# A two-layer attention trunk on one core: the opening's four hand-written orders replaced, nine modulation rows on TensorE instead of twelve, x in six loads instead of five

## The chip, the core and the metric

The kernel runs on one core of a Trainium2 chip. The core has a matrix engine (TensorE, PE in the profile, with its weight loads listed as PEld), a vector engine (DVE), a scalar engine (ACT), GpSimd (POOL) and a queue engine (SP), from which nearly all of this kernel's DMAs are issued. The metric is the device time of one execution in microseconds. It is compared with the time of the kernel before, run on the same chip.

## The reference

Two layers on 512 tokens of width 2048. The first is differential attention, the second forgetting attention on keys, values and gates that are projected once between them; each layer ends in a layer norm. All is float32. The change lies in the beginning of the first layer: its modulation, and the projection of its first two heads.

```python
def reference(x, c, w_mod, b_mod, ...):
    c_act = jax.nn.silu(c)
    for l in range(DEPTH):                                   # DEPTH = 2
        mod = c_act @ w_mod[l] + b_mod[l]                    # (1, 6144)
        shift, scale, gate = jnp.split(mod, 3, axis=-1)
        h = x * (1.0 + scale[:, None]) + shift[:, None]      # (1, 512, 2048)
        if l < N_A:
            y = diff_attention(h, a_w_in[l], a_w_out[l], ...)    # h @ w_in: 2048 to 8192, softmax, values, gate, @ w_out
        else:
            ...
            y = forgetting_attention(h, b_w_in[l - N_A], b_w_out[l - N_A], k_sh, v_sh, F_sh)
        x = layer_norm(DN_ALPHA * x + gate[:, None] * y, ln_g[l], ln_b[l])
    return x
```

`h` needs all 2048 rows of the first 4096 columns of `w_mod[0]` (33.6 MB) before its last column is there.

## The kernel before

A float32 product is made of three matmuls. Each operand is split into a high part, rounded to the matrix engine's faster 32-bit format, and the low rest: `hh` and `hl` for the activations, `whi` and `wlo` for the weights. A product is hh x whi + hl x whi + hh x wlo. ACT makes the high part of a weight block from its staged load (`wst` to `whi`, line 118), DVE the low part (`wlo`, line 125).

The opening is everything up to the end of the projections of heads 0 and 1. The 2048 rows of the contraction are 16 k-tiles of 128, and it does these things at once:

- The modulation. `sms` tiles hold pieces of `w_mod`, loaded on SP (step L, line 557). The k-tiles are grouped into nine sets: the first two hold one k-tile each, the other seven two. A set sums 16 blocks of 128 weight rows, here called rows. A row is either added on DVE into `sacc` (step d, lines 605 and 607) or multiplied on PE by the column `cact` straight into PSUM (step e, line 635, a group that a matmul of a zero mask opens, line 632). `PE_ROWS` says which rows are PE's. Once all rows of a set are there, PE sums `sacc` over the partitions into the same PSUM columns (step o, line 649) and DVE adds the bias: `mcol`, shift and scale (step m, line 660).
- The activations. `x` comes in quarters of 512 columns, the first in two parts (step X, line 567). PE transposes a k-tile (step t, line 675; the first into a bank called `px`), ACT applies scale and shift twice (`hh`, step h, line 683; `htmp`, step i, line 690), and DVE makes `hl` from the two (step l, line 698).
- The products. Weight blocks of two k-tiles are loaded on SP into four staging buffers (step W, line 59, two loads each), cast on ACT (step a) and finished on DVE (step b). Blocks of 384 columns and of 512 columns alternate for each head. A k-tile of a head is seven accumulations, three for the first block (banks called `sc` and `o` in the profile) and four for the second (`acc`), each of three matmuls, steps A (hh x whi), B (hl x whi) and C (hh x wlo), line 709: 672 in all. Both heads share seven PSUM banks and take turns in seven phases; ACT stores a bank's sums (step c, line 750) and loads them back (step r, line 759).
- Two matmuls of a constant tile (step F, line 621), whose result nothing reads.

What each of SP, ACT, PE and DVE does first and next is written out by hand in four strings (`ORDER_SP`, `ORDER_ACT`, `ORDER_PE`, `ORDER_DVE`): a letter is the next step of its kind, a number ahead of it repeats it. Steps that a string leaves out go to its end, as step p does in the kernel before (`load_parameters`, seven small loads of layer norm weights, lambda vectors and a gain that are used after the opening). Each engine runs its own string strictly in order and waits wherever something is not there yet. A modulation tile may be loaded when the tile five before it has been read (`NBUF`), a weight block when DVE is done with the block four before it.

After the opening the rest follows in program order: the remaining heads, the output projection, the shared keys and values, the second layer.

Of the kernel before, what the change touches and what calls it, by code (L numbers as in the profile page):

```python
# [16 lines left out]
P = 128  # L17
D = 2048
KT = D // P
T = 512  # L20
# [9 lines left out]

PHASES = [(0, 0, 2), (1, 0, 4), (0, 2, 6), (1, 4, 10), (0, 6, 14), (1, 10, 16), (0, 14, 16)]
KMAJOR = (0,)
PE_ROWS = {0: (2, 3, 6, 7), 1: (4, 5, 6, 7, 12, 13, 14, 15)}
EARLY = (0,)
NBUF = 5
ORDER_SP = '8LX4LW4LXW2LW4LW3LW2LW5L2W2LX2W4LW4LW3LW2LW3LXWLWLW2L2W5LWLW4LWLWLXW3LWL2WL2WL6W'
ORDER_ACT = 'haiahia5ca2cahiahi3c2rara2c2r2c2rahiahica2c2rc2r2c2rcahirahi2ahihia2cac3ra3c2rc2rahi2ahiahaihi2acrcrcra2crc2racrahihi3a2crc2rcarcr2c2r7c'
ORDER_PE = 'F4eFto3eAeA4eBoAtBCB2ACBACBACB2ACBC3ABC2B2AC2B3CAB2C3ABACBABABC3B2AC2BCA2CoBAtCACBA2C2Bt3ACAB3AB2CA4B2CBCACBCBCB2CAB2C3ABCACBA3BCABC4A3BoCA2CABA3CA2B2CB2At3AB2C2BCtCABA2B5AC2BA2C3BCA2C2B2CBAB2ACB3CBCA2CBCBABC2ACoB2ABABACtBCAB2ACBCtBAC2BC2ABCBAB2C2ABABACB2CB4A2B2CA2CBCABA3B2CAoABt3CBC2A2CBAtAC4BABCACA2CAB3ABCA2CBACBABACA2B2CA3BCA2CABACAC2BC2BABC2A2BACABCB2A2Bo2AC2AtCBACBCBC2ACA2BACA2BABCBCA2CBCA2C3BACACBCtAB2CA2B2ACABABCACAoCACA2C3BABCBtBCBA2BCA3CBAtBAB2C4A2C2ABCACB2CABA2BACAB2CB2A2BC2BACB4CBCAB3ACBABABC2B2CB2CAB2ACBCAB2C2ABABCBA2CB2ABABAoBCBAt2ACAC2AB3C2BABAt2B3CA4BACABA3CACABAB3CBCBAB4CA2BAB2A3CBA2BACBA2CBC2A2BC2A2B2A3CABCBACBA2B3ABAB3C2B5CABACBC'  # L40
ORDER_DVE = '13dm2dbl5dmb2dbl14dbm4dlbdl2db9dbdb2dmdbl3dldb10dmb5db3dldbl5dbm2dbl2dl4db2db6db3dm6dbdb2dl4dlb3dmb3db2ld2bdb3db5dmlbl4b'
MANUAL = {ET.DVE, ET.PE, ET.Activation, ET.SP}
CUT = False
LAM_INIT = 0.8 - 0.6 * math.exp(-0.0)
# [93 lines left out]
def tile_yoco(  # L138
# [44 lines left out]
    def acc_bank(name="acc"):  # L183
        return ps.tile([P, 512], F32, name=name, tag="acc", bufs=4)
# [4 lines left out]
    def tr_bank(name="tr"):  # L189
        return ps.tile([P, 512], F32, name=name, tag="tr", bufs=1)  # L190
# [105 lines left out]
    first = {h: (Job(a_w_in, [(256 * h, 256), (2048 + 256 * h, 128)]), vg[h]) for h in range(2)}  # L296
    kk = Job(a_w_in, [(2048 + 128, 128), (2048 + 384, 128)])

    sets = [(0, 1), (1, 1)] + [(k, 2) for k in range(2, KT, 2)]
    phases = PHASES  # L300
    kj = [Job(kv_w, [(512 * g, 512)]) for g in range(4)]

# [174 lines left out]
    with tc.tile_pool(name="start", bufs=2, reuse_waits="tile") as sp, tc.manual_schedule(engines=MANUAL):  # L477
# [5 lines left out]
        for i, (k0, nk) in enumerate(sets):  # L483
            nr = 8 // nk
# [2 lines left out]

        loads = []
        for n, (i, k, nr) in enumerate(tiles):
            step = nr // 2 if i < 2 else nr  # L490
            loads += [(n, kq, step, v) for kq in range(0, nr, step) for v in range(2)]
        xloads = [(0, 0, P), (0, P, T), (1, 0, T), (2, 0, T), (3, 0, T)]
        rows_pe = [tuple(PE_ROWS.get(i, ())) for i in range(len(sets))]
        e_list = [(i, k) for i in range(len(sets)) for k in rows_pe[i]]
        d_list = [(i, k) for i in range(len(sets)) for k in range(KT) if k not in rows_pe[i]]
# [2 lines left out]
        prods = []  # L498
        for n, (u, k0, k1) in enumerate(PHASES):
            for k in range(k0, k1, 2):  # L500
# [24 lines left out]
        cnt = dict.fromkeys("LXWpdmlbahicretoABCF", 0)  # L525
# [136 lines left out]
            return True  # L662

        def op_t(kt):
            if cnt["X"] <= (0 if kt == 0 else kt // 4 + 1):
                return False
            if kt in EARLY:
                px = acc_bank("px")
            else:
                if state["tr"] is not None:  # L670
                    return False
                px = tr_bank()
                state["tr"] = "x", kt
            for b in range(TB):
                PE.transpose(px[:, b * P : (b + 1) * P], xts[kt // 4][:, b, (kt % 4) * P : (kt % 4 + 1) * P], ident)
            pxs[kt] = px
            return True
# [76 lines left out]
        def op_r(j):  # L754
# [30 lines left out]
        kinds = ("LXWp", "ahicrK", "etoABCF", "dmlb")  # L785
# [626 lines left out]
    for i, (half, s) in enumerate(lag):  # L1412
# [304 lines left out]
```

## Time and profile before

| | us |
|---|---|
| median of three runs | 1938.87 (1938.58 to 1939.20) |
| profiled execution, its own time | 1938.17 |
| its span, first to last instruction | 1936.4 |
| PE busy in the span | 1915.8 |
| PE idle up to 42.2 | 8.0 |
| PE idle from 42.2 to 192.4 | 0.0 |
| PE idle from 192.4 to 1924.7 | 0.9 |
| after PE's last instruction | 11.7 |

A row of the timeline gives start and length in us, the engine (an engine's name with q is its issue queue), the line of the kernel, the operation, what it writes and reads by the program's names, the partitions and elements, and a count where several like instructions stand in a row; brackets hold the idle time ahead of it and what ended it. A matmul's length overlaps the next one's, since they are pipelined: what a matmul costs is the distance between two starts. In the trace each small float32 matmul and transpose stands as one or two instructions, so that a modulation row of one k-tile, two matmuls in the program, is four.

### The profile page before, as it was taken

How to read it: one execution, taken by the hardware profiler on the slowest of the kernel's cores; microseconds unless marked ns; L12 is line 12 of the kernel's file. 1: busy time of each engine (PE TensorE's matmuls, PEld its weight loads, DVE VectorE, ACT ScalarE, POOL GpSimd, SP SyncE). 2: the span in 40 equal slices, each digit the busy share in tenths (PEclk: the TensorE clock that was granted, in tenths of full speed). 3: DMA queues.
4: the chain of work that ended last, by engine and by line, in shares of the span. 5: the costliest groups of instructions: out<-in, count | busy, mean ns of one | idle time of the engine just before them, and what ended most of it. 6: DMA issues, size and time to landing. Idle time of an engine off the chain costs nothing.

```text
span 1936.4 us, 25779 instructions
## 1 busy us (share of the span) xinstructions
PE 1915.8 (99%) x8941; PEld 1598.8 (83%) x8941; DVE 1359.3 (70%) x2546; ACT 730.8 (38%) x1250; POOL 2.2 (0%) x10
## 2 busy tenths in 40 slices
PE   8999999999999999999999999999999999999997
PEld 7888888888888888888888898888888888888886
DVE  6884588777776768667675477677566666687657
ACT  3556444323333334531272232224343434353123
POOL 0000000000000000000000000000000000000000
PEclk9999999999999999999999999999999999999999
DMA  9993466676767675376547586774354555554622
GB/s 339 384 303 116 149 186 205 211 229 190 239 191 231 198 234 170 125 239 222 181 165 254 183 289 212 256 255 158 119 155 148 153 154 155 154 170 158 218 95 102
DMA packets 351630, 382.19 MB, mean 197 GB/s; under 512 B 77926, under 2 KB 255740, under 8 KB 350732
## 3 DMA queue, kind: packets, MB, share of 16 engines
q1 hardware_dynamic: 348620, 376.35, 60.7%
q10 hardware_dynamic: 2880, 4.20, 0.6%
q8 instruction: 70, 1.15, 0.2%
q14 instruction: 60, 0.49, 0.1%
HBM read 348.65 MB, written 31.80 MB: 196 GB/s over the span
## 4 chain that ended last, share of the span: by engine, by line
PE 81%; DVE 1%; issue 0%; DVEq 0%; ACT 0%
PE acc L201 25%; PE acc L202 25%; PE acc L203 25%; PE o L201 1%; PE o L202 1%; PE o L203 1%; PE sc L203 1%; PE sc L202 1%; PE sc L201 1%; PE sc L1299 0%; DVE wlo L107 0%; PE sc L209 0%; PE sc L208 0%; DVE hl L1309 0%; DVE z L1682 0%
## 5 line engine op out<-in xcount | busy, mean ns | idle before, releaser
L106 ACT CAST whi<-wst 128x1024 fp32r<-128x1024 f32 (+2 forms) x298 | 303.4, 1019 | 642.1 <-PE acc L203 342.7
L107 DVE TENSOR_TENSOR wlo<-wst,whi 128x1024 fp32r<-128x1024 f32 (+2 forms) x298 | 351.3, 1180 | 244.2 <-ACT whi L106 237.6
L201 PE MATMUL acc<-hh,whi 128*128 128x512 f32 x1184 | 463.5, 392 | 0.0
L202 PE MATMUL acc<-hl,whi 128*128 128x512 f32 x1184 | 461.7, 390 | 0.0
L203 PE MATMUL acc<-hh,wlo 128*128 128x512 f32 x1184 | 461.0, 390 | 0.0
L201 PE MATMUL acc<-whi,hh 128*128 128x512 f32 (+1 forms) x1168 | 443.4, 380 | 0.0
L202 PE MATMUL acc<-wlo,hh 128*128 128x512 f32 (+1 forms) x1168 | 441.5, 378 | 0.0
L203 PE MATMUL acc<-whi,hl 128*128 128x512 f32 (+1 forms) x1168 | 441.1, 378 | 0.0
L426 DVE SCALAR_TENSOR_TENSOR macc<-ms,cact,macc 128x512 f32<-128x512 f32 x307 | 229.0, 746 | 58.8 <-DMA ms<-in_w_mod_dram 41.3
L203 PEld LDWEIGHTS acc<-hh,wlo 128*128 128x128 f32 x1184 | 222.3, 188 | 47.9
L201 PEld LDWEIGHTS acc<-hh,whi 128*128 128x128 f32 x1184 | 222.4, 188 | 43.3 <-issue 0.6
L202 PEld LDWEIGHTS acc<-hl,whi 128*128 128x128 f32 x1184 | 222.5, 188 | 42.1
L203 PEld LDWEIGHTS acc<-whi,hl 128*128 128x128 f32 x1168 | 219.2, 188 | 41.2
L201 PEld LDWEIGHTS acc<-whi,hh 128*128 128x128 f32 x1168 | 219.2, 188 | 39.4 <-DVE ztmp L1207 0.4
L202 PEld LDWEIGHTS acc<-wlo,hh 128*128 128x128 f32 x1168 | 219.3, 188 | 38.8 <-DVE wlo L107 0.4
L607 DVE SCALAR_TENSOR_TENSOR sacc<-sms,cact,sacc 128x512 f32<-128x512 f32 (+1 forms) x123 | 87.5, 712 | 7.3 <-DMA sms<-in_w_mod_dram 4.0
L893 ACT ACTIVATE e<-e,mn 128x128 f32<-128x128 f32 (+3 forms) x64 | 36.0, 563 | 114.4 <-DVE mn L889 105.4
L1522 ACT ACTIVATE eb<-eb,mnb 128x128 f32<-128x128 f32 (+1 forms) x64 | 36.0, 562 | 83.8 <-DVE mnb L1519 83.0
L125 DVE TENSOR_TENSOR wlo<-wst,whi 128x768 fp32r<-128x768 f32 (+1 forms) x32 | 34.8, 1088 | 17.3 <-ACT whi L118 8.6
L709 PE MATMUL acc<-whi,hh 128*128 128x512 f32 x128 | 46.3, 394 | 0.0
L709 PE MATMUL acc<-whi,hl 128*128 128x512 f32 x128 | 45.9, 394 | 0.0
L889 DVE CUSTOM_DVE_ANT_0 e<-sc,bias 128x256 f32<-128x256 f32 (+2 forms) x48 | 26.5, 552 | 27.3 <-PE sc L203 27.2
(280 smaller groups left out, 1996.9 us busy)
## 6 DMA issues: line engine op xcount, KB each, us to landing
wst<-in_a_w_in_dram SPq DMA_DIRECT2D x240, 256.0 KB, 3.9
ms<-in_w_mod_dram SPq DMA_DIRECT2D x136, 256.0 KB, 4.1
ms<-in_kv_w_mod_dram SPq DMA_DIRECT2D x64, 512.0 KB, 3.9
wst<-in_b_w_in_dram SPq DMA_DIRECT2D x128, 256.0 KB, 2.8
sms<-in_w_mod_dram SPq DMA_DIRECT2D x56, 512.0 KB, 7.5
wst<-in_kv_w_dram SPq DMA_DIRECT2D x56, 512.0 KB, 4.2
ms<-in_w_mod_dram SPq DMA_DIRECT2D x32, 512.0 KB, 4.4
wst<-in_a_w_out_dram SPq DMA_DIRECT2D x32, 512.0 KB, 4.1
```

Of the source, the lines that this page charges most:

```text
L106: self.nc.scalar.copy(hi[:, :, :w], st[:, :, :w])
L107: self.nc.vector.tensor_tensor(lo[:, :, :w], st[:, :, :w], hi[:, :, :w].bitcast(F32), op=ALU.subtract)
L125: self.nc.vector.tensor_tensor(lo[:, :, :w], st[:, :, :w], hi[:, :, :w].bitcast(F32), op=ALU.subtract)
L201: PE.matmul(dst, lhs[0], rhs[0], start=start, stop=False)
L202: PE.matmul(dst, lhs[0], rhs[1], start=False, stop=False)
L203: PE.matmul(dst, lhs[1], rhs[0], start=False, stop=stop)
L426: ins = V.scalar_tensor_tensor(acc, w, cact[:, kt : kt + 1], acc, op0=ALU.mult, op1=ALU.add)
L607: V.scalar_tensor_tensor(acc, w, sc, acc, op0=ALU.mult, op1=ALU.add)
L709: PE.matmul(bank[n, bk], l, r, start=start, stop=stop, skip_group_check=True)
L889: V.tensor_tensor_reduce(out=e[:, :w], in0=sc[:, :w], in1=bias, scale=-1.0, scalar=3.0e38, op0=ALU.add, op1=ALU.min, accum_out=mn,)
L893: S.activation(e[:, :w], e[:, :w], AF.Exp, bias=mn, scale=-1.0, accum_out=rs)
L1522: S.activation(e[:, :w], e[:, :w], AF.Exp, bias=mn, scale=-1.0, accum_out=rs)
```

## The change

The table of the order is replaced whole, and a few numbers with it:

- `PE_ROWS`: set 0 keeps four rows on PE (0, 2, 5, 8 instead of 2, 3, 6, 7), set 1 has five (1, 2, 6, 12, 15) instead of eight. DVE has three rows more.
- `XLOADS`: the first quarter of x comes in three parts (128, 128 and 256 columns) instead of two (128 and 384); `x_last` tells each transpose which part it needs.
- `SETS` and `HALVES` give names to what was written in place; their values are the old ones, so the first two k-tiles are still summed one by one.
- The two F matmuls are gone. The tile that they read is still written.
- Step p stands ahead of the last eight loads of SP's string (one modulation piece and seven weight blocks) instead of behind them.
- The four strings are new.

```diff
+SETS = [(0, 1), (1, 1), (2, 2), (4, 2), (6, 2), (8, 2), (10, 2), (12, 2), (14, 2)]
+HALVES = (0, 1,)
+XLOADS = [(0, 0, 128), (0, 128, 256), (0, 256, 512), (1, 0, 512), (2, 0, 512), (3, 0, 512)]
 PHASES = [(0, 0, 2), (1, 0, 4), (0, 2, 6), (1, 4, 10), (0, 6, 14), (1, 10, 16), (0, 14, 16)]
 KMAJOR = (0,)
-PE_ROWS = {0: (2, 3, 6, 7), 1: (4, 5, 6, 7, 12, 13, 14, 15)}
+PE_ROWS = {0: (0, 2, 5, 8), 1: (1, 2, 6, 12, 15)}
 EARLY = (0,)
 NBUF = 5
-ORDER_SP = '8LX4LW4LXW2LW4LW3LW2LW5L2W2LX2W4LW4LW3LW2LW3LXWLWLW2L2W5LWLW4LWLWLXW3LWL2WL2WL6W'
...
+ORDER_SP = '8LX2LW3LW3LX3LW3LW3LWXLWLW3LW2LWLX3LWLW4LW3LW2LW2LWXLW4LWLW4L3W2LW5LWLXLWL2W2L2WLpWL6W'
...
-    sets = [(0, 1), (1, 1)] + [(k, 2) for k in range(2, KT, 2)]
+    sets = SETS
...
-            step = nr // 2 if i < 2 else nr
+            step = nr // 2 if i in HALVES else nr
...
-        xloads = [(0, 0, P), (0, P, T), (1, 0, T), (2, 0, T), (3, 0, T)]
+        xloads = XLOADS
+        x_last = [max(j for j, (q, f0, f1) in enumerate(xloads) if q == kt // 4 and f0 <= kt % 4 * P) for kt in range(KT)]
...
-            if cnt["X"] <= (0 if kt == 0 else kt // 4 + 1):
+            if cnt["X"] <= x_last[kt]:
                 return False
```

The lines of the new kernel stand three or four below the old ones. PE, from the mask matmul that opens set 1 to the transpose of the second k-tile, before (`sms` with `cact` are modulation rows, two matmuls each; `ones` with `sacc` is the column sum of a set; line 709 is products):

```order
L632 MATMUL tr<-mask,ident 128x2
L635 MATMUL tr<-cact,sms 128x1 x6
L709 MATMUL sc<-hh,whi 128x512
L635 MATMUL tr<-cact,sms 128x1 x2
L709 MATMUL sc<-hh,whi 128x512
L635 MATMUL tr<-cact,sms 128x1 x8
L709 MATMUL sc<-hl,whi 128x512
L649 MATMUL tr<-ones,sacc 128x1 x2
L709 MATMUL o<-hh,whi 128x512
L675 MATMUL tr<-ident,xt 128x128 x4
```

and the same stretch of PE now (lines 636, 639, 713, 653 and 679):

```order
L636 MATMUL tr<-mask,ident 128x2
L639 MATMUL tr<-cact,sms 128x1 x4
L713 MATMUL sc<-hh,whi 128x512
L639 MATMUL tr<-cact,sms 128x1 x2
L713 MATMUL sc<-hl,whi 128x512
L713 MATMUL sc<-hh,whi 128x512
L713 MATMUL sc<-hl,whi 128x512
L713 MATMUL o<-hh,whi 128x512
L713 MATMUL acc<-whi,hh 128x512 x2
L713 MATMUL o<-hl,whi 128x512
L713 MATMUL acc<-whi,hl 128x512
L639 MATMUL tr<-cact,sms 128x1 x2
```

Three rows stood ahead of the first product and two stand there now; the four behind the second product are gone, and eight products follow each other, among them those of the second weight block (`acc`) on the first k-tile. Behind what is shown come one more product, one row, set 1's column sums, two products and the transpose.

SP, from the first modulation pieces to the second weight block and the second part of x, before (`sms` are modulation pieces, 0.26 MB each where the row says 128x4x128; `wst` halves of weight blocks; `xt` parts of x):

```order
L557 DMA sms<-in_w_mod_dram 128x4x128 x8
L567 DMA xt<-in_x_dram 128x4x128
L557 DMA sms<-in_w_mod_dram 128x4x128 x4
L59 DMA wst<-in_a_w_in_dram 128x2x256
L59 DMA wst<-in_a_w_in_dram 128x2x128
L557 DMA sms<-in_w_mod_dram 128x4x128 x4
L567 DMA xt<-in_x_dram 128x4x384
L59 DMA wst<-in_a_w_in_dram 128x2x256 x2
```

and now:

```order
L561 DMA sms<-in_w_mod_dram 128x4x128 x8
L571 DMA xt<-in_x_dram 128x4x128
L561 DMA sms<-in_w_mod_dram 128x4x128 x2
L62 DMA wst<-in_a_w_in_dram 128x2x256
L62 DMA wst<-in_a_w_in_dram 128x2x128
L561 DMA sms<-in_w_mod_dram 128x4x128 x3
L62 DMA wst<-in_a_w_in_dram 128x2x256 x2
L561 DMA sms<-in_w_mod_dram 128x4x128 x3
L571 DMA xt<-in_x_dram 128x4x128
```

The first weight block stands two pieces earlier, the second one three pieces and a whole part of x earlier, and set 1's last three pieces behind it instead of ahead of it.

DVE, from set 0's rows to the columns of set 1 (`mcol`), before:

```order
L607 SCALAR_TENSOR_TENSOR sacc<-sms,cact,sacc 128x2x128 x11
L605 TENSOR_SCALAR sacc<-sms,cact 128x2x128
L660 TENSOR_TENSOR mcol<-tr,bcol 128x2
L607 SCALAR_TENSOR_TENSOR sacc<-sms,cact,sacc 128x2x128 x2
L125 TENSOR_TENSOR wlo<-wst,whi 128x2x384
L698 TENSOR_TENSOR hl<-htmp,hh 128x512
L607 SCALAR_TENSOR_TENSOR sacc<-sms,cact,sacc 128x2x128 x5
L660 TENSOR_TENSOR mcol<-tr,bcol 128x2
```

and now:

```order
L611 SCALAR_TENSOR_TENSOR sacc<-sms,cact,sacc 128x2x128 x11
L664 TENSOR_TENSOR mcol<-tr,bcol 128x2
L609 TENSOR_SCALAR sacc<-sms,cact 128x2x128
L128 TENSOR_TENSOR wlo<-wst,whi 128x2x384
L611 SCALAR_TENSOR_TENSOR sacc<-sms,cact,sacc 128x2x128
L702 TENSOR_TENSOR hl<-htmp,hh 128x512
L611 SCALAR_TENSOR_TENSOR sacc<-sms,cact,sacc 128x2x128 x9
L664 TENSOR_TENSOR mcol<-tr,bcol 128x2
```

Set 0 has as many rows on DVE as before. Set 1 has eleven (one, one and nine) instead of eight, nine of them behind the first `hl`.

More of the change, by code (lines that the diff above doesn't have):

```diff
@@ L39 @@
-ORDER_ACT = 'haiahia5ca2cahiahi3c2rara2c2r2c2rahiahica2c2rc2r2c2rcahirahi2ahihia2cac3ra3c2rc2rahi2ahiahaihi2acrcrcra2crc2racrahihi3a2crc2rcarcr2c2r7c'
-ORDER_PE = 'F4eFto3eAeA4eBoAtBCB2ACBACBACB2ACBC3ABC2B2AC2B3CAB2C3ABACBABABC3B2AC2BCA2CoBAtCACBA2C2Bt3ACAB3AB2CA4B2CBCACBCBCB2CAB2C3ABCACBA3BCABC4A3BoCA2CABA3CA2B2CB2At3AB2C2BCtCABA2B5AC2BA2C3BCA2C2B2CBAB2ACB3CBCA2CBCBABC2ACoB2ABABACtBCAB2ACBCtBAC2BC2ABCBAB2C2ABABACB2CB4A2B2CA2CBCABA3B2CAoABt3CBC2A2CBAtAC4BABCACA2CAB3ABCA2CBACBABACA2B2CA3BCA2CABACAC2BC2BABC2A2BACABCB2A2Bo2AC2AtCBACBCBC2ACA2BACA2BABCBCA2CBCA2C3BACACBCtAB2CA2B2ACABABCACAoCACA2C3BABCBtBCBA2BCA3CBAtBAB2C4A2C2ABCACB2CABA2BACAB2CB2A2BC2BACB4CBCAB3ACBABABC2B2CB2CAB2ACBCAB2C2ABABCBA2CB2ABABAoBCBAt2ACAC2AB3C2BABAt2B3CA4BACABA3CACABAB3CBCBAB4CA2BAB2A3CBA2BACBA2CBC2A2BC2A2B2A3CABCBACBA2B3ABAB3C2B5CABACBC'
@@ L41 @@
-ORDER_DVE = '13dm2dbl5dmb2dbl14dbm4dlbdl2db9dbdb2dmdbl3dldb10dmb5db3dldbl5dbm2dbl2dl4db2db6db3dm6dbdb2dl4dlb3dmb3db2ld2bdb3db5dmlbl4b'
+ORDER_SP = '8LX2LW3LW3LX3LW3LW3LWXLWLW3LW2LWLX3LWLW4LW3LW2LW2LWXLW4LWLW4L3W2LW5LWLXLWL2W2L2WLpWL6W'
+ORDER_ACT = 'ahiahia5ca2cahiahiacrcrcrcar2c2rcrahihia3ca3rcrcacrc2rhiahi2ahihiacra2c2racr2c2rcr3ahihi2ahiahia2c2rcr2crcrac2r3ahihaiacracrcrcrcr2c2r7c'
+ORDER_PE = '4eto2eAeBAB3A2BeBeoCAtAB3C2ACACB2ABCBC2BACAB2CABCBABCBACACACA2BCBA2B5A3BABCABC2Bo2Ct6C2ACtBAC2BCAC5A2BCBACBC2AB2CA2BABCABCB2C2AC2BABCABC2BC2ABCACBAC2B2CAoABAt2CABCBCBt2ACA2B3CABC2ABCB2AC3ABABCA2B2CBC2BCBAC2ABCA2CBABA2CA3B2C2ABoBA2Bt5ACBC2B2CtBC2ACACA2CBC2BCBCABA2BACA2B2C3A2BAB2AC3Bo2CtA2CB2C2AtA3C2B2A2CA2BCACB2ABCBCBA2BCACBAC2ABCABCACBACBCAC2BCABA2CBCB2ABA2C2A3BAC2A2BAoC2BA4C2BCABAt3ABCBA2CB3ABCA2CACBtCBAB2ABCBACBC2BACAC2A2BA4CoBA2BCtBABCBCACACAC2BABAt2CABABAB2ACBABABA4CBCAC2BCBC3A2CBACBAC2B2CA2BACAC3BAB3CACB2ABCBCA2B2ABAC3ABCBCBCB2C2ABAC2B2AC2ABCo2A2CAtACBC2BC2BCBACACBtA2CBAC2AB2ABA2CA4BCABA2CA2CBCBCBACBABC2BCB2A2CACBA2BC2A2BA2BC2ACB2CACBACACACBCBCABA2B3CBC'
@@ L42 @@
+ORDER_DVE = '12dmdbdl9dmb2dl2db12dbmb2dldbl3db9dbdmb2dl3dl2db6db3dbdm5dlb3dl7dbmbl2dl3db5db3db5db2dm3db2dl4dl2dbdm2dbdblbl2db4dbdb6dbmblbl2b'
 MANUAL = {ET.DVE, ET.PE, ET.Activation, ET.SP}
```

## The prediction

> **What bounds the kernel now.** I read the page's busy shares first, then the busy time by stage, then the chain of waits, and last the timeline of the opening. The page:
>
> ```profile
> span 1936.4 us, 25779 instructions
> PE 1915.8 (99%) x8941; PEld 1598.8 (83%) x8941; DVE 1359.3 (70%) x2546; ACT 730.8 (38%) x1250; POOL 2.2 (0%) x10
> PE 81%; DVE 1%; issue 0%; DVEq 0%; ACT 0%
> ```
>
> PE is the bound: busy 99% of the span, and 81% of the chain that ended last (third line, by engine). Where its idle 20.6 us lie is told by the busy time in seven stretches (length, then busy us of PE, PEld, DVE, ACT, POOL, the granted clock, DMA share, GB/s):
>
> ```profile
> 0.00:15.40 15.40, 7.99 (x30) 6.68 (x30) 7.06 (x21) 1.90 (x3) 1.60 (x9) 1.00 0.85 253
> 15.40:27.40 12.00, 11.95 (x49) 11.32 (x50) 7.09 (x13) 4.21 (x6) 0.00 (x0) 1.00 1.09 373
> 27.40:40.40 13.00, 13.00 (x58) 10.67 (x57) 11.40 (x16) 6.69 (x11) 0.00 (x0) 1.00 1.09 382
> 40.40:42.20 1.80, 1.26 (x10) 0.90 (x9) 1.76 (x2) 0.00 (x0) 0.00 (x0) 1.00 1.09 380
> 42.20:192.40 150.20, 150.20 (x714) 124.95 (x714) 110.81 (x152) 85.93 (x140) 0.56 (x1) 1.00 0.81 275
> 192.40:1924.70 1732.30, 1731.38 (x8086) 1444.26 (x8084) 1213.57 (x2332) 630.36 (x1089) 0.00 (x0) 1.00 0.59 188
> ```
>
> From 192.4, where the opening ends, to 1924.7 PE stands 0.92 us in 1732, and PE's instructions after the opening are the same ones in the same order in both kernels. So the change is worth what it moves the end of the opening, and no more. Inside the opening PE stands for 7.4 us before 15.4 and 0.54 us near 41; the rest is work.
>
> Busy does not mean fast, though. The timeline of the part in which the orders differ most (start, length, engine, line, tiles, count, and in brackets the wait before it):
>
> ```profile
> 9.04 0.67 PE L621 MATMUL fb<-fill 128*128 128x384 f32 x1
> 10.00 4.13 DVE L607 SCALAR_TENSOR_TENSOR sacc<-sms,cact,sacc 128x256 f32<-128x256 f32 x8 [1.18 <-DMA sms<-in_w_mod_dram]
> 12.22 1.12 PE L675 MATMUL px<-ident,xt 128*128 128x128 f32 x4 [2.52 <-DMA xt<-in_x_dram]
> 14.19 1.01 PE L649 MATMUL tr<-ones,sacc 128*128 128x1 f32 x4 [0.85 <-DVE sacc L607]
> 15.23 0.16 DVE L660 TENSOR_TENSOR mcol<-tr,bcol 128x2 f32<-128x2 f32 x1 [0.84 <-PE tr L649]
> 15.45 0.59 PE L632 MATMUL tr<-mask,ident 128*128 128x2 f32 x2 [0.25 <-DVE mcol L660]
> 15.90 2.70 PE L635 MATMUL tr<-cact,sms 128*128 128x1 f32 x12
> 16.23 1.43 SPq L59 DMA_DIRECT2D wst<-in_a_w_in_dram  x2
> 18.46 0.77 PE L709 MATMUL sc<-hh,whi 128*128 128x512 f32 x1
> 18.63 2.56 DVE L607 SCALAR_TENSOR_TENSOR sacc<-sms,cact,sacc 128x256 f32<-128x256 f32 x5
> 19.74 0.77 PE L709 MATMUL sc<-hh,whi 128*128 128x512 f32 x1
> 20.31 3.41 PE L635 MATMUL tr<-cact,sms 128*128 128x1 f32 x16
> 22.70 1.04 ACT L118 CAST whi<-wst 128x1024 fp32r<-128x1024 f32 x1 [4.91 <-DMA wst<-in_a_w_in_dram]
> 23.58 0.77 PE L709 MATMUL sc<-hl,whi 128*128 128x512 f32 x1
> 24.15 0.85 PE L649 MATMUL tr<-ones,sacc 128*128 128x1 f32 x4
> 24.86 0.77 PE L709 MATMUL o<-hh,whi 128*128 128x512 f32 x1
> 25.03 0.16 DVE L660 TENSOR_TENSOR mcol<-tr,bcol 128x2 f32<-128x2 f32 x1 [3.85 <-PE tr L649]
> 25.43 1.05 PE L675 MATMUL tr<-ident,xt 128*128 128x128 f32 x4
> 26.14 0.78 PE L709 MATMUL sc<-hl,whi 128*128 128x512 f32 x1
> 26.71 0.63 PE L709 MATMUL sc<-hh,wlo 128*128 128x512 f32 x1
> 27.14 0.45 PE L709 MATMUL o<-hl,whi 128*128 128x512 f32 x1
> 27.42 0.62 PE L709 MATMUL acc<-whi,hh 128*128 128x512 f32 x2
> ```
>
> Three prices stand here. A modulation row on PE is four instructions; the twelve from 15.90 to 18.46 make three rows in 2.56 us, 0.853 each. A product costs 0.43 (26.71 to 27.14). And at about 27.2 PE's pace doubles. Much later it is
>
> ```profile
> 159.16 0.39 PE L709 MATMUL acc<-whi,hh 128*128 128x512 f32 x1
> ...
> 162.11 0.39 PE L709 MATMUL sc<-hh,whi 128*128 128x512 f32 x1
> ```
>
> with thirteen products from one to the other: 2.95/13 = 0.227 a product. The granted clock reads 1.00 throughout, so the slow pace shows only in the starts. Between 15.45 and 27.2 PE thus gets through eight rows (6.8 us), the mask matmul (0.45), set 1's column sums (0.85), a transpose (0.85) and only some six and a half products.
>
> **The change part by part.**
>
> *One row fewer on DVE behind the third pair of pieces.* DVE's eight rows from 10.00 on are rows 8 to 15, 0.516 each. With row 8 on PE, seven are left, and set 0's columns come 0.5 us earlier. Row 12 would start at 11.55 instead of about 12.08; whether its piece is there the trace does not show. The x load behind it, 0.26 MB more, landed at 12.22. At the 331 GB/s of that stretch,
>
> ```profile
> 10.00:15.00 5.00, 1.93 (x8) 1.53 (x8) 4.14 (x9) 0.00 (x0) 0.00 (x0) 1.00 1.09 331
> 15.00:20.00 5.00, 4.75 (x21) 4.57 (x22) 3.82 (x8) 2.29 (x3) 0.00 (x0) 1.00 1.08 348
> ```
>
> that is 0.8 us after the piece, which then was there at 11.4. Bounds 0 and 0.52; I take 0.5, since both rows give it.
>
> *Three rows fewer on PE.* Set 1 has five rows on PE instead of eight: 3 x 0.853 = 2.56 us. DVE takes three more at about 0.51, 1.5 us, inside the 3.85 us in which it waits ahead of 25.03; without that hole they would cost 1.5. With the 0.5 above, PE has 3.06 us more before 27.2 for slow products: 3.06/0.43 = 7.1 products, each later worth 0.227. **1.6 us.** This needs fourteen products before 27.2, and there are that many only if the second weight block is there (next part).
>
> *Loads moved.* The second weight block (issued from 16.23, waited for until 22.7) now has 1.5 MB less ahead of it in SP's queue: three of set 1's pieces and all of x's second load, 0.79 MB each. At 348 to 373 GB/s that is 4.2 to 4.5 us, so it lands at about 18.3 and its cast of 1.04 ends at about 19.4. Set 1's last pieces had that block and the x load, 1.3 MB, behind them, so they landed 3.4 us ahead of 22.7 at 382 GB/s, near 19.2; now the block's 0.5 MB stands ahead of them, 1.5 us, and they come at about 20.7. PE's rows that use them are placed behind eight products, DVE's are its last. Bounds for the block: 18.3 and, if the earlier issue gives nothing, 22.6 as before (the last rival).
>
> Six x loads instead of five are one more issue on SP, 0.7 us by the nearest row (half of 1.43), while the transfers run at 373 to 382 GB/s and stay behind SP: I take nothing, 0.7 at most. The seven small parameter loads go ahead of the last eight loads of SP's order instead of behind them all, at most 7 x 0.7 = 5 us in front of seven weight blocks and one piece. SP's own waits there,
>
> ```profile
> SPq L59 <- DVE wlo L125: 52.0, 17, 10.2
> ```
>
> 52 us in 17 times at the weight loads (L59) until DVE has freed a staging buffer, are the cover: SP issues these blocks when it may, not when it can. Nothing, then; without the cover those blocks, and the products on them, come up to 5 us late.
>
> *The walk.* Columns of set 0 at 14.7, mask at 14.95, two rows to 17.1, product one (18.46 before), a row to 18.4, then eight products in a row, 0.43 each, to 21.8, a row, a product, a row, set 1's sums.
>
> *The pace.* Before 23.58 there are two products in eight microseconds, and rows back to back leave the pace slow; 3.6 us after 23.58, with nearly half of that time products, it doubles. In the new order such a stretch begins at 18.4, so I put the doubling at 18.4 + 3.6 = 22.0. What took 5.2 us (22.0 to 27.2) then takes 0.227/0.43 = 0.53 of it. **2.4 us.** Lower bound 0 (it stays at 27.2), upper at 20.4, where the stretch from 17.1 holds as many products: 6.8 x 0.47 = 3.2.
>
> [...]
>
> The two fill matmuls stood in waits for data, so they count nothing; had they held PE up, dropping them would be a gain.
>
> *Waits for DVE.* The one old stall is here:
>
> ```profile
> 40.18 0.61 PE L709 MATMUL sc<-hh,wlo 128*128 128x512 f32 x2
> 41.33 1.02 PE L649 MATMUL tr<-ones,sacc 128*128 128x1 f32 x8 [0.54 <-DVE sacc L607]
> ```
>
> Two products from 40.18 end their issue at 40.63, so PE loses 0.70. With the opening earlier PE comes to each later column sum earlier, and DVE, 88% busy from 27.4 to 40.4, has to be earlier too. It mostly is, because it hangs on set 1's columns and those move, and its wait for the third weight block goes. I take 0.5 us lost over all later sums, between +0.7 (the old stall gone) and -1.2 (two more of its size).
>
> **Sum:** 1.6 + 2.4 - 0.5 = 3.5 us. The profiled execution took 1938.17 (span 1936.4, 1.77 around it) and would take 1934.7; the runs shown have a median of 1938.87, 0.7 longer, so the forecast for the median is 1938.87 - 3.5 = **1935.4**.
>
> **Rivals.**
>
> *The pace doubles sooner.* PE counts any stretch half full of products, so 17.1 to 20.4 is enough. For: the stretch ahead of 27.2 held no more. Against: one doubling in one trace. 1.6 + 3.2, less 0.3 in which rows 12 and 15 wait for pieces until 20.7, less 0.5: 4.0, **1934.9**. [...]
>
> *The pace stays.* The rows between the products keep it slow to 27.2. For: rows back to back did so from 15.9 to 23.6. Against: eight products on end are denser than anything before 27.2. 1.6 - 0.5 = 1.1: **1937.8**.
>
> *DVE becomes the bound.* If every later column sum stays where it was, PE waits at each. For: 88% busy, and the one stall. Against: 110.81 of 150.20 us later. By the last of the nine sums the new order has issued 559 products, the old 548 (counted in the orders), so even then 11 x 0.227 = 2.5 us stay: **1936.4**.
>
> *Slower: the second weight block is not early.* Four banks need it from the sixth product on, at 20.1. If it lands at 22.6 as before, its cast ends at 23.7 and PE stands 3.6 us in the middle of the stretch. Each us of that costs 0.53 (0.227/0.43), 1.9 against the 1.6, which alone is 1939.2; so from 3.0 us of standing on, a landing near 22, the change loses. And each us by which the doubling then falls behind 27.2 costs 0.47 more: if four products from 23.7 and what follows (two rows, sums, a transpose) do not make a stretch, the next begins at 30.2 and doubles 3.6 later, at 33.8: 6.6 x 0.47 = 3.1, **1942.3**. For: six microseconds of queue lie between issue and landing, so an earlier issue is no earlier landing where the queue is long. Against: it is long by bytes, and the bytes ahead are fewer.
>
> **How the numbers follow.** Forecast 0.50, sooner 0.23, pace stays 0.13, DVE 0.07, late weights 0.07. A measurement of this kernel can tell about 0.2%, 3.9 us, from no change, so faster means below 1935.0 and slower above 1942.7. Faster: a third of the forecast's own spread (1934.5 to 1936.3) and eight tenths of the sooner pace, 0.17 + 0.18, and 0.02 for both terms larger: 0.37. Slower: only late weights with more behind them, and what I do not see: 0.05. Range: the sooner pace with the old stall gone, 1933.7, to the pace that stays, 1937.8: 1933.6 to 1937.9.
>
> **What would show it.** Right: set 0's columns (mcol) near 14.7; the first product near 17.1; the second block's cast near 18.3; PE's starts 0.227 apart from about 22; the opening's end 3 to 4 us ahead of 192.4. Wrong: the doubling at 27 still (second term), a cast still at 22 (third part), PE waits for sacc of over 0.7 (the DVE term), or a stretch after 192 that is not the old one shifted.

## The result, and the profile after

| us | before | after |
|---|---|---|
| median | 1939.08 | 1935.13 |
| lowest to highest of 11 runs | 1938.44 to 1939.87 | 1932.87 to 1937.86 |
| profiled execution | 1938.17 | 1937.62 |
| its span | 1936.4 | 1935.8 |
| end of its opening | 192.33 | 191.59 |

The ratio is 0.9982 (95% interval 0.9974 to 0.9990), 3.5 us of 1939 and less than the 0.2% that the prediction called faster; the two medians lie 3.95 us apart. The median lies 0.3 us from the forecast. But two things in the table do not fit a change worth 3.5 us. The runs of after are spread over 5.0 us, those of before over 1.4; sorted, seven lie at 1932.9 to 1935.2, four at 1937.3 to 1937.9, and none between. And the execution that was profiled gained 0.55 us only.

The page of after, its first line, PE's busy time and the shares of the chain that ended last:

```profile
span 1935.8 us, 25766 instructions
...
PE 1915.7 (99%) x8927; PEld 1597.8 (83%) x8927; DVE 1360.6 (70%) x2549; ACT 731.8 (38%) x1250; POOL 2.2 (0%) x10
...
PE 81%; DVE 1%; issue 0%; DVEq 0%; ACT 0%
```

Nothing there tells it from before. The busy time of after in five stretches (columns as in the prediction):

```profile
0.00:14.90 14.90, 7.57 (x28) 6.36 (x28) 6.81 (x20) 1.90 (x3) 1.60 (x9) 1.00 0.84 246
14.90:31.10 16.20, 16.17 (x53) 13.94 (x54) 11.78 (x21) 5.39 (x7) 0.00 (x0) 1.00 1.11 373
31.10:191.60 160.50, 160.50 (x763) 133.48 (x762) 120.93 (x165) 92.11 (x148) 0.56 (x1) 1.00 0.83 284
191.60:1924.10 1732.50, 1731.44 (x8086) 1444.04 (x8085) 1213.55 (x2332) 630.75 (x1090) 0.00 (x0) 1.00 0.60 188
1924.10:1935.80 11.70, 0.00 (x0) 0.00 (x0) 7.53 (x14) 1.69 (x3) 0.00 (x0) 0.70 0.36 142
```

From 14.9 to the end of the opening PE stands for 0.03 us: the old stall near 41 is gone. Behind the opening PE's 8086 instructions take 1732.5 us, against 1732.3 before. The timeline of PE in the part that was reordered:

```profile
14.93 0.59 PE L636 MATMUL tr<-mask,ident 128*128 128x2 f32 x2 [0.25 <-DVE mcol L664]
15.38 1.85 PE L639 MATMUL tr<-cact,sms 128*128 128x1 f32 x8
17.09 0.77 PE L713 MATMUL sc<-hh,whi 128*128 128x512 f32 x1
17.66 0.85 PE L639 MATMUL tr<-cact,sms 128*128 128x1 f32 x4
18.37 0.77 PE L713 MATMUL sc<-hl,whi 128*128 128x512 f32 x1
...
21.93 0.85 PE L639 MATMUL tr<-cact,sms 128*128 128x1 f32 x4
22.64 0.77 PE L713 MATMUL acc<-whi,hl 128*128 128x512 f32 x1
23.21 0.85 PE L639 MATMUL tr<-cact,sms 128*128 128x1 f32 x4
23.91 0.99 PE L653 MATMUL tr<-ones,sacc 128*128 128x1 f32 x4
...
30.46 0.63 PE L713 MATMUL acc<-wlo,hh 128*128 128x512 f32 x1
30.89 0.44 PE L713 MATMUL acc<-whi,hl 128*128 128x512 f32 x1
31.16 0.62 PE L713 MATMUL acc<-whi,hh 128*128 128x512 f32 x2
31.61 0.39 PE L713 MATMUL sc<-hl,whi 128*128 128x512 f32 x1
```

Up to 22.6 this is the forecast's walk to a tenth of a microsecond: mask at 14.93, product one at 17.09, eight products from 18.37 to 21.93. What was forecast for 22.0, the doubling of the pace, is not there. A slow product has a length of 0.63, a fast one of 0.39; the product at 30.89 has 0.44, and those behind it start 0.227 apart. So the pace doubled at about 31.0, 3.7 us later than in the trace of before, and at 31.1 PE had started 23 products, in the trace of before 24. What the rows had won was given back there; the 0.74 us at the end of the opening are the old stall.

ACT's cast of the second weight block shows that the load was not late:

```profile
18.58 1.04 ACT L121 CAST whi<-wst 128x1024 fp32r<-128x1024 f32 x1 [1.47 <-DMA wst<-in_a_w_in_dram]
```

So the median was as forecast, and the one trace contradicts the largest term behind it. The experiments are about that term.

### The profile page after: what moved, and what is told of

Its sections match the earlier page's. It is cut to its first block, busy times and chain, and to the rows that moved or that the text cites. A ratio compares the mean times of both kernels' runs of the same rounds, so it can differ in the third digit from the quotient of the medians.

```text
span 1935.8 us, 25766 instructions
## 1 busy us (share of the span) xinstructions
PE 1915.7 (99%) x8927; PEld 1597.8 (83%) x8927; DVE 1360.6 (70%) x2549; ACT 731.8 (38%) x1250; POOL 2.2 (0%) x10
## 4 chain that ended last, share of the span: by engine, by line
PE 81%; DVE 1%; issue 0%; DVEq 0%; ACT 0%
PE acc L204 25%; PE acc L205 25%; PE acc L206 25%; PE o L204 1%; PE o L205 1%; PE o L206 1%; PE sc L206 1%; PE sc L205 1%; PE sc L204 1%; PE sc L1303 0%; DVE wlo L110 0%; PE sc L212 0%; PE sc L211 0%; DVE hl L1313 0%; DVE z L1686 0%
## 5 line engine op out<-in xcount | busy, mean ns | idle before, releaser
L713 PE MATMUL acc<-wlo,hh 128*128 128x512 f32 x128 | 46.6, 399 | 0.0
```

The source lines that it names most:

```text
L713: PE.matmul(bank[n, bk], l, r, start=start, stop=stop, skip_group_check=True)
```

## The experiments

Diffs of an order show the beginning of its string as far as it changes; where only its end changes, the whole. The time at which PE's pace doubles is read in each trace as above, from the one instruction whose length lies between the slow and the fast one.

**The changed kernel again.** No edit.

> The changed kernel unaltered, for a second trace and more times. Theory A (the time at which PE's pace doubles differs from execution to execution, and nothing else does): the doubling falls anywhere from 21 to 32 us; the profiled run's time lies on 1937.6 - 0.47 x (31.1 - doubling), within 0.5 us, so a doubling at 24 goes with 1934.3 and one at 27.7 with 1936.0; the walk up to the 14th product (27.045 in the first trace) is the same to 0.1 us as long as the pace has not doubled; the opening's end moves with the time of the run, the rest of the span (1744.2 us after it) does not. Rival B (loads land at different times, and PE or DVE wait for them): the doubling is at 31 again whatever the time, and the difference stands as waits of PE in front of products, rows or sums in the opening, or the length behind the opening changes.

Measured: 1934.15 median of 11 (1933.25 to 1938.84), ratio 0.9979 (0.9970 to 0.9988); three runs above 1937. The profiled execution took 1933.85. PE's timeline there:

```profile
19.75 1.05 PE L713 MATMUL acc<-whi,hh 128*128 128x512 f32 x2
20.61 0.49 PE L713 MATMUL o<-hl,whi 128*128 128x512 f32 x1
20.93 0.40 PE L713 MATMUL acc<-whi,hl 128*128 128x512 f32 x1
21.17 0.50 PE L639 MATMUL tr<-cact,sms 128*128 128x1 f32 x4
...
37.57 0.61 PE L713 MATMUL acc<-whi,hl 128*128 128x512 f32 x2
38.41 0.80 PE L653 MATMUL tr<-ones,sacc 128*128 128x1 f32 x6 [0.22 <-DVE sacc L611]
```

The same instructions in the same order, and the pace doubles at 20.8 (the product at 20.61 has 0.49). Ten microseconds earlier than in the first trace, at 0.47 us each (a product takes 0.227 at the fast pace and 0.43 at the slow one, 0.53 of it), are 4.8; the time is 3.8 us shorter, the opening 4.5 (it ends at 187.12). The stall at set 2's sums is back with 0.38 us, since two products that start at 37.57 are issued by 38.03. By the line that was expected of theory A the time would be 1932.8, 1.1 below what was measured: its 0.5 was too narrow, because the stall is back and because the part behind the opening differs by itself (the time of the run less the end of its opening is 1745.8 to 1747.7 us in the fourteen profiled executions of this study). The walk was not the same to 0.1 us either: product one came at 16.62 instead of 17.09. Rival B's doubling at 31 whatever the time is refuted. What makes the time of doubling differ was open.

**Fill matmuls in PE's waits**, in the changed kernel and in the one before:

```diff
-ORDER_PE = '4eto2eAeBAB3A2BeBeo
+ORDER_PE = '2e2F2e6FtFoF2eAeBAB3A2BeBeo
```

```diff
-ORDER_PE = 'F4eFto3eAeA4eBo
+ORDER_PE = 'F2eF2e8Ft2FoF3eAeA4eBo
```

> The changed kernel with ten fill matmuls (zeros, 384 columns) in waits that PE has anyway: two behind the second row of set 0, six behind the fourth in front of the first transpose, one behind that, one behind set 0's sums. Theory A: PE is then filled without a gap from about 10.2 to 13.5 us, the pace doubles there or soon after product one (13.5 to 20), the landing of loads and DVE set the opening from then on, and its end comes 3 to 5 us ahead of 191.6; time 1932.5 to 1934.0, all runs within 1.5 us. If the low work from 13.7 to 17.1 (sums, rows) lets the pace fall back, the doubling is seen early and again later, and the time is that of the changed kernel. Rival B: 1935.1 with the same spread of 5 us, wherever the doubling falls.

> The kernel before with twelve fill matmuls in PE's waits instead of two (eight in front of the first transpose, two behind it, one behind set 0's sums, one in front of row one and one behind row two). Theory A: the pace doubles before 20 us, but the old order then waits for DVE's sums of set 2 near 40 (1.7 us instead of 0.5 to 0.7) and for loads, so only 1 us is won: 1937.4 to 1938.2; the change would be worth 4 to 5.5 us between two filled kernels. Theory A2 (the opening hangs on the pace alone): 1935 or less, and the change worth 2 us as the rows alone. Rival B: 1939.1, unchanged.

Measured: the changed kernel with fills 1934.94 (1933.46 to 1938.36, three of eleven above 1937), ratio 0.9981 (0.9973 to 0.9990): nothing won, the same two groups, doubling in its trace at 22.6 and no earlier one, so theory A's 1932.5 to 1934.0 was missed. Before with fills (the edit has thirteen, one more than the expectation counts) 1938.07 (1937.40 to 1941.06), ratio 0.9997 (0.9988 to 1.0006): not told apart from before. That lies in theory A's range, but not for its reason: PE does not wait for set 2's sums in this trace, the pace fell back. PE's timeline, before with fills:

```profile
9.12 2.91 PE L621 MATMUL fb<-fill 128*128 128x384 f32 x8
11.83 1.06 PE L675 MATMUL px<-ident,xt 128*128 128x128 f32 x4
12.54 0.99 PE L621 MATMUL fb<-fill 128*128 128x384 f32 x2
13.54 0.79 PE L649 MATMUL tr<-ones,sacc 128*128 128x1 f32 x4
...
14.83 1.48 PE L635 MATMUL tr<-cact,sms 128*128 128x1 f32 x12
16.75 0.50 PE L709 MATMUL sc<-hh,whi 128*128 128x512 f32 x1 [0.45 <-ACT whi L118]
17.09 0.60 PE L635 MATMUL tr<-cact,sms 128*128 128x1 f32 x4
17.55 0.78 PE L709 MATMUL sc<-hh,whi 128*128 128x512 f32 x1
...
27.20 0.58 PE L709 MATMUL acc<-whi,hl 128*128 128x512 f32 x1
27.62 0.39 PE L709 MATMUL acc<-whi,hh 128*128 128x512 f32 x1
```

The pace doubles within the four column sums at 13.54 (0.79 instead of 1.0), three rows run in 1.48 instead of 2.7, and within the row at 17.09 it falls back: the product at 17.55 is slow again. It doubles the second time at 27.6. From starts one by one the three moments are 13.94, 17.34 and 27.61: 3.40 and 10.27 apart, the second about three times the first. The stretch before the first was fills and transposes, that before the fall nearly all rows and sums, with which PE was busy but for 0.45 us. The author's estimate from these numbers is that the pace changes at moments some 3.4 us or a multiple of it apart (a grid, in the expectations below), by what PE did just before. It rests on two distances in one trace; no run shows how the pace is set, and the next experiments try what follows from the estimate.

**The old loads.** The changed kernel with the old order of loads and the old five loads of x:

```diff
-ORDER_SP = '8LX2LW3LW3LX3LW3LW3LWX
+ORDER_SP = '8LX4LW4LXW2LW4LW3LW2LW
...
-XLOADS = [(0, 0, 128), (0, 128, 256), (0, 256, 512), (1, 0, 512), (2, 0, 512), (3, 0, 512)]
+XLOADS = [(0, 0, 128), (0, 128, 512), (1, 0, 512), (2, 0, 512), (3, 0, 512)]
```

> The changed kernel with the old order of loads and the old five x loads; rows and the other orders as changed. The forecast's part on the second weight block: it lands near 22.5 as before, its cast ends near 23.6, and PE stands about 2.9 us in front of the product that needs it; 1938.4 to 1941 by where the doubling falls (at 27.2: 1938.5; at 31.1: 1940.2). If the earlier issue of that block was worth nothing: no stand, 1935.1 as the changed kernel.

Measured: 1941.59 (1939.88 to 1942.94), ratio 1.0014 (1.0005 to 1.0022): slower than before. PE's timeline:

```profile
20.28 0.63 PE L713 MATMUL o<-hh,whi 128*128 128x512 f32 x1
23.40 1.22 PE L713 MATMUL acc<-whi,hh 128*128 128x512 f32 x2 [2.49 <-ACT whi L121]
...
32.10 1.01 PE L713 MATMUL sc<-hh,whi 128*128 128x512 f32 x2
32.94 0.39 PE L713 MATMUL acc<-wlo,hh 128*128 128x512 f32 x1
```

From 20.28 to 23.40 PE issues one product of 0.43 us, so it stands 2.7 us for the second block's cast, in the middle of the stretch, and the doubling comes at 32.9. Product one also waits 0.66 us, at 17.44, since the first block is late too and ACT makes `hh` behind its cast. The time is 0.6 above the range expected, which ended with a doubling at 31.1. The new order of PE without the new order of loads loses. The edit puts back all of SP's order; the wait for the second block, 2.49 us by its row, is the longest that PE has in this trace from 17.4 to 35.

**One long run of products, and products strewn.** By now the theory, an estimate from the distances above and from the doublings at 20.8, 22.6 and 31.0 with the same order of products, was: these moments lie differently in each execution, and only a stretch dense in products and transposes doubles the pace. If so, the order of PE decides in how many executions it doubles early. Two orders with the same instructions and loads, the first and then the second:

```diff
-ORDER_PE = '4eto2eAeBAB3A2BeBeoCAtAB3C2ACACB2
+ORDER_PE = '4eto2e3A3B3A2BA3eoCtB3CAACACB2
```

```diff
-ORDER_PE = '4eto2eAeBAB3A2BeBeoCAtAB3C2ACACB2
+ORDER_PE = '4eto2eAeBAB2AeAe3BoCAtAB3CAACACB2
```

> The changed kernel's PE order with the first products in one unbroken run: eleven products behind the second row of set 1, then the three rows that stood among them, then the sums. Same loads, same rows, same number of instructions. Theory C, formed on the traces so far: the pace is set anew every 3.4 us on a grid that lies differently in each execution; it doubles where PE spent some three quarters of such a stretch on products or transposes. The changed kernel's eight products on end are caught by some grids (doubling at 20.8, 22.6) and missed by others, which then wait until 31. A run of eleven, 4.7 us from 17.1 on, is caught by every grid: the doubling falls between 19.5 and 23 in all executions, the runs near 1937 to 1939 are gone, all runs between 1933 and 1936 and the median near 1934, about 1 us below that of the changed kernel in the mean. Rival D (two states of the chip that have nothing to do with the order of PE): three runs in ten stay at 1937 to 1939. Rival E (the three rows later make set 1's columns and what hangs on them late): median 1935.5 or more, with PE's waits in front of products behind 24 us.

> The other way: the changed kernel with its two later rows strewn among the products, so that no more than five products stand on end before set 1's sums. Same loads, rows and number of instructions. Theory C: no stretch of 3.4 us before 24.8 is dense enough, every execution doubles between 28 and 31.5, and all runs lie where the slow ones of the changed kernel lie: 1937.0 to 1939.0, median near 1938, so the change would be worth nothing. Rival D: seven runs in ten stay at 1933 to 1935.

(The run has twelve products, 16.65 to 22.18, not eleven; PE waits 0.26 us in it for the second block's cast.) Measured: the run 1934.07 (1933.77 to 1934.67, ten runs), ratio 0.9974 (0.9964 to 0.9983); strewn 1937.13 (1935.84 to 1938.61, eleven runs), ratio 0.9991 (0.9982 to 1.0000). PE's timeline with the run:

```profile
16.65 1.20 PE L713 MATMUL sc<-hh,whi 128*128 128x512 f32 x2
...
21.75 0.63 PE L713 MATMUL acc<-whi,hh 128*128 128x512 f32 x1
22.18 1.67 PE L639 MATMUL tr<-cact,sms 128*128 128x1 f32 x12
23.71 0.58 PE L653 MATMUL tr<-ones,sacc 128*128 128x1 f32 x4
```

and strewn:

```profile
27.82 0.63 PE L713 MATMUL o<-hh,wlo 128*128 128x512 f32 x1
28.24 0.48 PE L713 MATMUL acc<-wlo,hh 128*128 128x512 f32 x1
28.57 0.63 PE L713 MATMUL sc<-hh,whi 128*128 128x512 f32 x2
```

The doubling is at 22.7 with the run (three rows in 1.67, neither 2.7 nor 1.5) and at 28.5 strewn. With the run the late group is gone and the spread falls from 5.6 us to 0.9; strewn, the early group is gone, though four runs at 1935.8 to 1936.7 lie under the 1937.0 that was expected, and no trace shows when the pace doubled in those. Two states of the chip that do not ask for the order of PE (rival D) would have left three in ten late and seven in ten early; they are refuted: both kernels were timed together on one chip, and the highest time with the run, 1934.67, lies below the lowest strewn, 1935.84. So is rival E: behind 24 us the trace with the run lists no wait of PE in the opening.

**Three rows back on PE**, in the kernel with the run:

```diff
-PE_ROWS = {0: (0, 2, 5, 8), 1: (1, 2, 6, 12, 15)}
+PE_ROWS = {0: (0, 2, 5, 8), 1: (1, 2, 4, 5, 6, 7, 12, 15)}
...
-ORDER_PE = '4eto2e3A3B3A2BA3eo
+ORDER_PE = '4eto5e3A3B3A2BA3eo
-ORDER_DVE = '12dmdbdl9dm
+ORDER_DVE = '12dmdbdl6dm
```

> The run of eleven, with three rows of set 1 (4, 5 and 7) back on PE in front of product one, and off DVE: eight rows on PE as before. The forecast's second term: three rows at 0.853 us, 2.56 us of slow products, worth 1.4 us (2.56 x 0.53) at the same time of doubling. Theory C: the run also begins 2.56 us later, so the doubling falls between 22 and 25.4 instead of 19.5 and 23, and the sum is 2.5 us: median near 1936.5. If the pace doubled for another reason at the same time as in the run of eleven: 1935.4. If rows on DVE cost as much as rows on PE: 1934.

Measured: 1936.37 (1935.24 to 1937.52), ratio 0.9988 (0.9979 to 0.9996): 2.3 us over the run alone. In its trace product one starts at 19.48 instead of 16.65 and the pace doubles at 23.6 instead of 22.7; the opening ends 1.80 us later, 1.4 for the rows and 0.9 x 0.47 = 0.4 for the doubling.

**The rest of the loads**, in the kernel with the run: first both, then the small loads alone.

```diff
-XLOADS = [(0, 0, 128), (0, 128, 256), (0, 256, 512), (1, 0, 512), (2, 0, 512), (3, 0, 512)]
+XLOADS = [(0, 0, 128), (0, 128, 512), (1, 0, 512), (2, 0, 512), (3, 0, 512)]
...
-ORDER_SP = '8LX2LW3LW3LX3LW3LW3LWXLWLW3LW2LWLX3LWLW4LW3LW2LW2LWXLW4LWLW4L3W2LW5LWLXLWL2W2L2WLpWL6W'
+ORDER_SP = '8LX2LW3LW3LX3LW3LW3LWLWLW3LW2LWLX3LWLW4LW3LW2LW2LWXLW4LWLW4L3W2LW5LWLXLWL2W2L2WLWL6W'
```

> The run of eleven, with the small parameters' loads behind all others as they were not in the forecast's costing at nothing but as the diff's last word has it undone: the p of the table goes to the end, and x comes in five loads instead of six (the second and third of x's first block as one). The forecast put both at nothing: the same median as the run of eleven within 0.5 us. If x's larger load delays the pieces behind it (0.5 MB, 1.4 us at 373 GB/s): rows or sums of set 1 wait, at most 1 us: 1935.

> The run of eleven with one thing of the last experiment alone: the small parameters' loads behind all others; x stays in six loads. In the trace with both undone, DVE waited 0.52 us for a piece of set 2 near 36 and 0.19 us near 25, and PE reached set 2's sums 0.40 us later, while SP issued everything from 20 us on 1.4 us later. If that is x's larger load, as its 0.5 MB at 373 GB/s suggest, this kernel has the time of the run of eleven: 1934.1 within 0.3 us. If the place of the small loads is what cost: 1935.0.

Measured: both 1935.03 (1934.38 to 1935.90), ratio 0.9980 (0.9971 to 0.9988); the small loads last alone 1934.55 (1933.60 to 1935.33), 0.9978 (0.9969 to 0.9987). Both together cost about 1 us. With both, on DVE and on PE:

```profile
36.51 3.12 DVE L611 SCALAR_TENSOR_TENSOR sacc<-sms,cact,sacc 128x512 f32<-128x512 f32 x4 [0.52 <-DMA sms<-in_w_mod_dram]
```

```profile
39.77 1.02 PE L653 MATMUL tr<-ones,sacc 128*128 128x1 f32 x8 [0.21 <-DVE sacc L611]
```

DVE waits for a piece of set 2 and PE for DVE. In the trace with the run DVE waits 0.2 us for a piece from 10 to 40, and PE, there and in the trace with the small loads alone, not at all for these sums. The place of the small loads alone costs 0.5 us in the median, with ranges that overlap: not settled. The wait points to x's larger part for the rest, but the two kernels that would tell them apart, 1935.03 and 1934.55, overlap as well and were timed on different chips, so how the 1 us divides stays open.

**One row fewer on PE than the change.** Row 6 of set 1 on DVE, in the kernel with the run:

```diff
-PE_ROWS = {0: (0, 2, 5, 8), 1: (1, 2, 6, 12, 15)}
+PE_ROWS = {0: (0, 2, 5, 8), 1: (1, 2, 12, 15)}
...
-ORDER_PE = '4eto2e3A3B3A2BA3eo
+ORDER_PE = '4eto2e3A3B3A2BA2eo
-ORDER_DVE = '12dmdbdl9dm
+ORDER_DVE = '12dmdbdl10dm
```

> The run of eleven with one more row of set 1 (row 6) on DVE: four on PE, two of them behind the run. In its trace DVE ended set 1's rows at 22.2 us and then waited 2.0 us for PE's sums, which came at 23.7. If that wait is cover for the 0.51 us of a row, PE saves a row at the fast pace, 0.45 us, in most executions (0.85 in those that double late): 1933.5. If DVE's 0.51 us come back later at set 2's sums, where DVE is just in time: 1934.1, nothing won.

Measured: 1934.72 (1933.23 to 1936.76), ratio 0.9977 (0.9968 to 0.9986). Nothing is won, and the median is 0.6 above the higher of the two times expected; PE's 0.2 us of waiting for `sacc` are back in its trace, and 0.3 for a weight block. One of the ten runs, at 1936.76, lies 1.6 us above the others; whether its pace doubled late no trace shows.

**Third and second traces of the two kernels.** No edit.

> The kernel before once more, for a second trace. Theory C: its stretches dense enough begin only at 23.6, so the doubling falls between 27.2 and 30.7 whatever the grid, its runs lie within 1.6 us, and the time is 1938.2 + 0.47 x (doubling - 27.3). A doubling ahead of 26, or a time that does not follow it within 0.5 us, speaks against C.

> The changed kernel a third time, for a third trace. Theory C: the doubling falls in 20.5 to 22.5, or in 27.3 to 31; with the first the time is 1933.3 to 1935.2, with the second 1936.5 to 1938.8. A doubling between 23.5 and 27, or an early one with a late time, speaks against C.

Measured: before 1938.99 with the doubling at 29.6 (1939.3 by the line expected), after 1935.14 with the doubling at 22.4. Neither speaks against theory C. But that the time of before follows the line is luck. Its opening ended where the first one did (192.39 and 192.33), and the 0.8 us lie behind it. PE at set 2's sums in that trace:

```profile
40.92 0.61 PE L709 MATMUL sc<-hh,wlo 128*128 128x512 f32 x2
41.38 0.94 PE L649 MATMUL tr<-ones,sacc 128*128 128x1 f32 x8
```

There is no wait. The doubling 2.3 us later costs 1.1, the stall that is not there saves 0.7, and product one at 17.81 instead of 18.46 saves 0.3: together 0.1. So in these two traces the stall goes with the earlier doubling: PE had issued what stands ahead of the sums by 40.63 in the first, by 41.38 in the second. The third trace of after lies 1.6 us above theory A's line, and its part behind the opening is 1.7 longer than in the first trace. That the runs of before lie within 1.6 us did not come true either: the 85 timed beside the experiments lie at 1937.8 to 1940.9, with one at 1942.7, in no two groups. All profiled executions together, with the runs of the same kernel beside them:

| kernel | profiled, us | pace doubles at | opening ends at | runs, us |
|---|---|---|---|---|
| before | 1938.17 | 27.3 | 192.3 | 1937.8 to 1940.9 and 1942.7 |
| before, again | 1938.99 | 29.6 | 192.4 | |
| after | 1937.62 | 31.0 | 191.6 | 1932.9 to 1935.2 and 1937.2 to 1938.8 |
| after, again | 1933.85 | 20.8 | 187.1 | |
| after, third | 1935.14 | 22.4 | 187.4 | |
| after, fills | 1934.55 | 22.6 | 187.7 | 1933.5 to 1938.4 |
| before, fills | 1937.40 | 13.9, back 17.3, 27.6 | 191.2 | 1937.4 to 1941.1 |
| after, old loads | 1941.14 | 32.9 | 194.3 | 1939.9 to 1942.9 |
| run | 1934.64 | 22.7 | 188.0 | 1933.8 to 1934.7 |
| strewn | 1937.13 | 28.5 | 190.4 | 1935.8 to 1938.6 |
| run, eight rows | 1936.37 | 23.6 | 189.8 | 1935.2 to 1937.5 |
| run, loads undone | 1934.66 | 22.3 | 188.4 | 1934.4 to 1935.9 |
| run, small loads last | 1934.13 | 20.7 | 187.3 | 1933.6 to 1935.3 |
| run, four rows | 1933.40 | 20.9 | 187.6 | 1933.2 to 1936.8 |

Of the changed kernel's 23 runs 16 lie in the early group, 7 in the late one; of 32 runs with the run of twelve and five rows on PE none lies above 1935.9. The kernel with the run is the better one: its mean is 1934.22, that of the changed kernel 1935.28, and it has no late executions. The two were timed on different chips, on which the medians of before lie within 0.2 us of each other (1938.74 to 1938.90).

How dense a stretch has to be, the traces do not show. In the first trace of before the 3.56 us from 23.58 to 27.14 are products and transposes for 2.85 us, 0.80 of it from start to start, and the pace doubled at 27.3. In the first trace of after products alone fill the 3.56 us from 18.37 to 21.93, and the pace stayed slow until 31.0; behind the same products it doubled at 20.8 and 22.4. So the share by itself does not say when the pace doubles, and the three quarters of theory C stay an estimate: neither the share nor what counts in it was tried by itself.

## Why the prediction was right, and where it was not

**Rows: right.** Product one came at 17.09 (17.1 predicted), the mask at 14.93 (14.95), set 0's columns at 14.72 (14.7). That the times agree to a tenth is luck: in the other two traces of after product one came at 16.62 and 16.81, in the other trace of before at 17.81 instead of 18.46, with the first transpose of x earlier too. What stays is the distance from the mask to product one, 2.15 to 2.16 us now and 3.01 before in every trace of the two kernels, which is the one row fewer ahead of it. Three rows were put at 2.56 us of slow products, worth 1.4 of the 1.6; putting them back moved the opening by 1.80 with 0.4 of it from the doubling.

**The second weight block: right.** Its cast began at 18.58 (18.3), and without the early load PE stood 2.7 us (3.6 by the rival). That rival's price, up to 1942.3 with the doubling at 33.8, is near what the old loads gave: 1941.59, doubling at 32.9, though some of it is the first block and the other loads that were put back too.

**The other loads: a size too small.** They were put at nothing. Undoing both cost 1 us in the kernel with the run.

**The pace: the step that failed.** "I put the doubling at 18.4 + 3.6 = 22.0" took the 3.6 us of one execution for a delay that begins with the dense stretch. The traces show no such delay. The changed kernel's eight products on end begin at 17.90, 18.09 and 18.37 in its three traces and last 3.56 us at the slow pace; the pace doubled at 20.8, 22.4 and 31.0, which is 2.9, 4.3 and 12.6 us behind their start. Against 27.3 the first two are worth 3.1 and 2.3 us, and the third loses 1.7. No trace shows the 20.4 of the upper bound: 20.8 is the earliest of the three. What the prediction gave as three cases with chances of their own (forecast, sooner, stays) are outcomes of one kernel, in one execution or the next. The median was right because 16 of 23 executions are early. That it came within 0.3 us of the forecast is luck, since it lies between executions whose openings won 5.2 and 0.7 us. Only six of the 23 lie in the forecast's own spread of 1934.5 to 1936.3; most of the early ones are below it, and the late group is the rival of the pace that stays, at 1937.2 to 1938.8 instead of 1937.8.

**Fill matmuls: right.** More of them bought nothing that the runs tell from no change, in either kernel; leaving out the old two was not tried by itself. In the one trace in which the pace doubled behind them, at 13.94, it fell back at 17.34, behind 3.40 us of nearly all rows and sums.

**Waits for DVE: not as forecast.** 0.5 us lost was taken between +0.7 and -1.2. The stall at set 2's sums is 0.70 and 0 in the two traces of before and 0, 0.38 and 0 in the three of after. Against the trace that the forecast started from, the term is a gain of 0.3 to 0.7; against the other one it is 0 to 0.4 lost. So it goes by the execution, and no loss of 0.5 was seen. In set 1 DVE's three rows more cost PE nothing: they ended before PE asked for them. DVE did not become the bound.

**The sum, by execution,** against the first trace of before. Early (the second trace): 1.6 for the rows, 6.5 x 0.47 = 3.1 for the pace, 0.3 for the stall, and 0.2 because the walk ran 0.47 us ahead in that execution (product one at 16.62): 5.2. The opening ended 5.21 earlier. Late (the first trace): 1.6 - 1.7 + 0.7 = 0.6; it ended 0.74 earlier.

## What to carry to other kernels

Where a stage starts at a slow pace, try an order in which its products stand in one long run: here, by their times, 16 of 23 executions were early with 3.56 us of products on end and 32 of 32 with 5.5 us (five rows on PE in both). Small one-column matmuls went before or behind that run; with rows strewn among the products the median was 1937.13 instead of 1934.07. Where runs of one kernel fall into two groups, take a second and a third trace and compare one event in them before explaining a difference: here one trace of each kernel showed the change as worth half a microsecond. A time that falls on an expected line is not yet its cause: compare the stage too, as in the second trace of before. A term for an event that comes at another time in each execution (20.8, 22.4 and 31.0 here) has a spread, and its mean depends on how many executions have the event early.

## What was not expected of the hardware

The pace fell back 3.40 us after it had doubled, while PE had one gap of 0.45 us in its records; the work was nearly all one-column matmuls (13.54 to 17.5 in the trace of before with fills). The granted clock does not show the pace: in the first trace of after it read 1.00 from 14.9 to 31.1, where the pace was slow but for the last 0.1 us, and 1.00 from 31.1 to 191.6, where it was fast. And from the end of the opening to the end of the run the same work took 1745.8 to 1747.7 us. Between the two early traces of after that makes 1.0 of the 1.3 us by which they differ; what causes it stays open.
